# A pool of their own for the last split weights of FFN 1, and the second head's context keys right behind the first head's

## The chip, the cores and the metric

The kernel runs on one core of a Trainium2 chip. The metric is the device time of one execution in microseconds (us). The kernel before took 988.46 us (median of 3 runs, 988.08 to 989.26).

## What is computed

One block over 256 latent tokens (stream x) and 256 context tokens (stream ctx), 1024 channels, float32. The parts that matter here:

```
x   = x   + 0.5 * g1x * swiglu(modulate(rmsnorm(x,   norm_ffn1), sh1x, sc1x), w13_ffn1, w2_ffn1)
ctx = ctx + 0.5 * g1c * swiglu(modulate(rmsnorm(ctx, norm_ffn1), sh1c, sc1c), w13_ffn1, w2_ffn1)
qc, kc, vc, ... = project(modulate(rmsnorm(ctx, norm_mix), sh2c, sc2c), w_in)
qx, kx, vx, ... = project(modulate(rmsnorm(x,   norm_mix), sh2x, sc2x), w_in)
qx, kx = rope_2d(qx, rows), rope_2d(kx, rows)
```

Then come 4 heads of bidirectional retention of the latent queries over context and latent keys, a Fourier branch, a merge, a second FFN on x, and a final norm.

## The kernel before, in words

**Products in three terms.** Each float32 operand is split into a high part (rounded to fp32r) and a low part (the rest). `mm3` (lines 93 to 97) adds three matmuls: low weight by high activation (L95), high by low (L96), high by high (L97). `load_w` (line 77) fetches a chunk of weights (128 x up to 1024) into a raw tile `wr`, ScalarE casts it to `wh` (L85), and VectorE, or GpSimd where the caller asks for it, subtracts to give `wl` (L86). The tags `wr`, `wh` and `wl` have 4 buffers each, so 4 chunks at most are held in split form at one time. `split` (line 89) does the same two steps (L90, L91) for a given destination.

**FFN 1, second half** (`ffn1_down(1, g)`, line 472). Eight feature blocks j are made, each by 33 matmuls of 512 columns with 11 split blocks of weights, which come in two chunks (6 and 5 blocks). The last two, j = 6 and 7, are kept back (`late`) and run stream by stream: for the context columns j = 6 then 7, then for the latent columns j = 6 then 7, 33 matmuls of 256 columns each. So their four split chunks stay in the `wh` and `wl` buffers until the end of this stage, which are all four of each. They are put 16 columns into their buffers (`at`). The norm of the context stream (`stage2_norm(0)`: six matmuls with a matrix of ones, L506 and L508, a square root on ScalarE, L233, a reciprocal on VectorE, L235) is set in after the first blocks of the latent columns.

**Start of the mixers** (lines 857 to 867). `stage2_mod(0, ...)` makes the context's activations `h2ch`/`h2cl` block by block: VectorE multiplies by the norm (L328, writes `xr`), ScalarE adds the shift (L331, the high part), VectorE subtracts (L332, the low part). `first_unit` projects the first head's context keys (tile `kc`, 48 matmuls of 256 columns) and transposes the activations (tile `ht`, L631) block by block. Its hook, after block `HOOK` = 0, emits the latent stream's norm and its 8 activations `h2xh`/`h2xl`. Then `first_unit` does the same for the latent keys (`kx`), `project` makes the first head's queries (`q`), and the second head's latent keys (`kx1`). `k_weights(0)` and `q_weights(0)` give their subtractions to GpSimd (`G`), those of later heads to VectorE.

**The head loop** (lines 869 to 890). For the first head: scores (`s`, 24 matmuls), the second head's latent keys are rotated, then the second head's context keys are projected (line 884, tile `kc`, 48 matmuls), then `u_unit` (which needs the scores after their evacuation into `pt`), then the second head's queries (`q1`), then `o_unit`. `q_evac` (line 717) rotates and splits the queries (L705, L709, L90, L91); the scores need it.

**What sets the order.** Only the opening is ordered by hand. After it, the framework orders each engine's instructions when the kernel is built: by program order as the priority, by readiness in a model of the engines, and by free buffers. The order is then fixed, and each engine works through it and waits where it must.

**Memory.** Pools on the "left" and on the "right" side are two stacks that grow towards each other. In each partition, `gp` on the left ends at byte 178,208, and above it lay `adp` and `adr`, which are closed before this stage. On the right, `dp` ends downward at 206,304, and `mc` (the 16 tiles of 1,024 bytes of `h2ch`/`h2cl`) takes 189,920 to 206,304. A tile that lies over an older one waits for that one's last reader (`reuse_waits="tile"`).

Of the kernel before, what the change touches and what calls it, by code (L numbers as in the profile page):

```python
# [8 lines left out]
F32R = mybir.dt.float32r  # L9
# [4 lines left out]
P = 128  # L14
T = 256
D = 1024
KT = D // P
# [7 lines left out]
HALF = MT // 2  # L25
# [1 line left out]
RAW = 4  # L27
OUT = (P, KT, T)
UB = 4
HOOK = 0  # L30
LINE = 32
TC_KW = dict(schedule_with_timeline_sim=True)

# [6 lines left out]
def block_kernel(ctx: ExitStack, tc: tile.TileContext, i: dict, out: bass.AP):  # L40
    nc = tc.nc
# [10 lines left out]
    def fpool(stack, name, side):  # L52
        return stack.enter_context(tc.tile_pool(name=name, bufs=1, reuse_waits="tile", side=side))
# [7 lines left out]
    def shifted(pool, name, eighths):  # L61

        if eighths:
            V.memset(pool.tile([P, 8 * eighths], F32, name=name), 0.0)

    def bank(name):
        return psum.tile([P, 512], F32, name=name, tag="ps")

    def f32(ap):
        return ap.bitcast(F32)  # L70

    uid = [0]

    def wtile(t, name):
        return wp.tile([P, 1024], F32 if t == "wr" else F32R, name=name, tag=t, bufs=4)

    def load_w(src, n, lo_engine=None, at=0):

        uid[0] += 1
        raw, hi, lo = [wtile(t, f"{t}{uid[0]}")[:, at : at + n] for t in ("wr", "wh", "wl")]  # L80
        dst = raw
        if len(src.shape) == 3:
            dst = dst.rearrange("p (k c) -> p k c", k=src.shape[1])
        nc.sync.dma_start(dst, src)
        S.copy(hi, raw)  # L85
        (lo_engine or V).tensor_tensor(lo, raw, f32(hi), op=ALU.subtract)  # L86
        return hi, lo

    def split(dst_hi, dst_lo, src):
        S.copy(dst_hi, src)  # L90
        V.tensor_tensor(dst_lo, src, f32(dst_hi), op=ALU.subtract)  # L91

    def mm3(o, w, a, start, stop):

        PE.matmul(o, w[1], a[0], start=start, stop=False)  # L95
        PE.matmul(o, w[0], a[1], start=False, stop=False)  # L96
        PE.matmul(o, w[0], a[0], start=False, stop=stop)  # L97

    def sl(pair, *idx):
        return pair[0][idx], pair[1][idx]  # L100
# [13 lines left out]
    pools = {}  # L114
# [227 lines left out]
    def gated_unit(pa, pb, name):  # L342
        sa = tp.tile([P, 512], F32, name=f"sa{name}", tag="t2k", bufs=T2K)
        S.activation(sa, pa, AF.Silu)
        V.tensor_tensor(sa, sa, pb, op=ALU.mult)
        gg = (
            gp.tile([P, 512], F32R, name=f"gh{name}", tag="gh", bufs=HALF),
            gp.tile([P, 512], F32R, name=f"gl{name}", tag="gl", bufs=HALF),
        )
        split(gg[0], gg[1], sa)  # L350
        return gg
# [74 lines left out]
    def some_ada(n):  # L426
        for _ in range(min(n, len(todo))):
            ada(*todo.pop(0))

    def ffn1_up(m):  # L430
# [10 lines left out]
                mm3(ps, sl(ws[k // 4], slice(None), slice(c, c + P)), h[k], k == 0, k == KT - 1)  # L441
        return gated_unit(pa, pb, f"1_{m}")

    def w2_chunks(src, kts, at=0):
        ws, k0 = [], 0
        for n in kts:
            w = load_w(src[:, k0 * P : (k0 + n) * P], n * P, at=at)
            ws += [sl(w, slice(None), slice(c * P, (c + 1) * P)) for c in range(n)]
            k0 += n
        return ws  # L450
# [3 lines left out]
    def add_sq(ap, cols, first, name):  # L454

        sq = tp.tile([P, 512], F32, name=f"sq{name}", tag="t2k", bufs=T2K)
        w = cols.stop - cols.start
        if first:
            S.activation(ssum[0][:, cols], ap, AF.Square)
            return  # L460
        S.activation(sq[:, :w], ap, AF.Square)
        V.tensor_tensor(ssum[0][:, cols], ssum[0][:, cols], sq[:, :w], op=ALU.add)

    def y_evac(ps, j, streams, st, col0):
        for n, s in enumerate(streams):
            c = slice(s * T, (s + 1) * T)
            V.scalar_tensor_tensor(
                xs[j][:, c], ps[:, col0 + n * T : col0 + (n + 1) * T], gate_col(st, s, j),
                xs[j][:, c], op0=ALU.mult, op1=ALU.add,
            )  # L470

    def ffn1_down(hf, gs, n_ada=0):
        late = []
        if hf:
            ssum[0] = per.tile([P, 512], F32, name="ssum2", tag="ssum")
        for j in range(KT):
            some_ada(n_ada)
            in_two = hf and j >= KT - 2
            ws = w2_chunks(i["w2a"][hf, j], (6, 5), 16 if in_two else 0)
            if in_two:  # L480
                late.append((j, ws))
                continue
            ps = bank(f"y{hf}_{j}")
            for k in range(HALF):
                mm3(ps, ws[k], gs[k], k == 0, k == HALF - 1)
            y_evac(ps, j, (0, 1), 0, 0)
            if hf:
                add_sq(xs[j], slice(0, 512), j == 0, f"2_{j}")
        for s in (0, 1):
            for j, ws in late:  # L490
                ps = bank(f"y{hf}_{j}_{s}")
                c = slice(s * T, (s + 1) * T)
                for k in range(HALF):
                    mm3(ps[:, :T], ws[k], sl(gs[k], slice(None), c), k == 0, k == HALF - 1)
                    if (s, j, k) == (1, KT - 2, 3):
                        norms.append(stage2_norm(0))
                y_evac(ps, j, (s,), 0, 0)
                sq = tp.tile([P, T], F32, name=f"sq2_{j}_{s}", tag="t1k", bufs=2)
                S.activation(sq, xs[j][:, c], AF.Square)
                late_sq[s].append(sq)  # L500
# [3 lines left out]
    def stage2_norm(s):  # L504
        ps = bank(f"st2_{s}")
        PE.matmul(ps[:, :T], ones, ssum[0][:, s * T : (s + 1) * T], start=True, stop=False)  # L506
        for n, sq in enumerate(late_sq[s]):
            PE.matmul(ps[:, :T], ones, sq, start=False, stop=(n == 1))  # L508
        return rstd_of(ps[:, :T], T, f"2_{s}")
# [17 lines left out]
    def log_sigmoid():  # L527
# [28 lines left out]
    hx2 = [  # L556
        (mp.tile([P, T], F32R, name=f"h2xh{k}"), mp.tile([P, T], F32R, name=f"h2xl{k}"))
        for k in range(KT)
    ]
# [4 lines left out]
    def decays(hd):  # L564
# [16 lines left out]
    raw = tp.tile([P, P], F32, name="unit_2", tag="t1k", bufs=2)  # L581
    nc.sync.dma_start(raw, i["unit"])
    V.tensor_copy(unit, raw)
    dec = {0: decays(0)}
    S.activation(warm, dec[0][0][:, :1], AF.Sqrt, bias=dec[0][1][:, :1])
    ffn1_down(1, g)
    ffn1.close()
    mc = fpool(heads, "mc", "right")
    hc2 = [
        (mc.tile([P, T], F32R, name=f"h2ch{k}"), mc.tile([P, T], F32R, name=f"h2cl{k}"))  # L590
        for k in range(KT)
    ]
# [23 lines left out]
    def stage2_mod(s, r):  # L616
        for k in range(KT):
            modulated((hc2, hx2)[s][k], 1, (s,), k, r, s * T, f"2_{s}_{k}", None)
# [21 lines left out]
    def first_unit(s, w, a, pss, hook=None):  # L640

        banks = {}
        for k in range(KT):
# [3 lines left out]
            transposed(s, k, banks)  # L647
            if hook and k == HOOK:
                hook()
# [42 lines left out]
    def k_weights(hd):  # L692
        return [load_w(i["wk"][hd, n], 1024, None if hd else G) for n in range(2)]

    def kc_evac(pss, at):
        for e in range(2):
            split(keys[e][0][:, :T], keys[e][1][:, :T], pss[e][:, at[e] : at[e] + T])
# [27 lines left out]
    def project(ws, a, name):  # L725
        ps = bank(name)
        pair_of(ws, a, (ps, ps), (0, T))
        return (ps, ps), (0, T)
# [128 lines left out]
    wk = k_weights(0)  # L857
    stage2_mod(0, norms[0])
    kc = [bank(f"kc0_{e}") for e in range(2)]
    first_unit(0, wk, hc2, kc, lambda: stage2_mod(1, stage2_norm(1)))  # L860
    kc_evac(kc, (0, 0))
    kx = [bank(f"kx0_{e}") for e in range(2)]
    first_unit(1, wk, hx2, kx)
    kx_evac(0, kx, (0, 0))
    q_evac(0, *project(q_weights(0), hx2, "q0"))
    wk = k_weights(1)
    kx = project(wk, hx2, "kx1")
    sq = None
    for hd in range(HEADS):
        last = hd == HEADS - 1  # L870
        score_unit(hd)
        if last:
            fourier_open()
            fourier_in(0)
        else:
            dec[hd + 1] = decays(hd + 1)
            if hd:
                wk = k_weights(hd + 1)
                kx = project(wk, hx2, f"kx{hd + 1}")
            kx_evac(hd + 1, *kx)  # L880
        if hd:
            o_norm(hd - 1, sq)
        if not last:
            kc_evac(*project(wk, hc2, f"kc{hd + 1}"))
        us = u_unit(hd)
        if last:
            fourier_in(1)
        else:
            q_evac(hd + 1, *project(q_weights(hd + 1), hx2, f"q{hd + 1}"))
        sq = o_unit(hd, us)  # L890
# [19 lines left out]
    for j in range(KT):  # L910
        ws = [load_w(i["wgate"][j, c], 1024) for c in range(2)]
# [6 lines left out]
        wr = [load_w(i["pret"][j, c], 1024) for c in range(2)]  # L918
        for k in range(2 * KT):
            c = (k % 8) * P  # L920
# [120 lines left out]
    for j in range(KT):  # L1041
        ws = w2_chunks(i["w2b"][j], (8, 8, 6))
# [6 lines left out]
        if j < KT - 1:  # L1049
            add_sq(xs[j][:, XC], slice(0, T), j == 0, f"4_{j}")  # L1050
            c = NRM + 3 * KT + j
# [5 lines left out]
    c = NRM + 4 * KT - 1  # L1057
# [109 lines left out]
```

## Time and profile before

| what | value |
|---|---|
| median of 3 runs | 988.46 us (988.08 to 989.26) |
| the profiled execution | 986.11 us |
| its span, first to last instruction | 984.3 us |
| TensorE matmul (PE) busy | 957.3 us, 97% |
| VectorE (DVE) busy | 658.1 us, 67% |
| ScalarE (ACT) busy | 468.1 us, 48% |
| GpSimd (POOL) busy | 37.7 us, 4% |
| chain that ended last, PE's share | 93% |

The span is 1.81 us shorter than the profiled execution's own time, and that execution is 2.35 us below the median. A row of the timeline gives the start and the duration in us, the engine, the line, the operation, the tile written and the tiles read, and in brackets how long the engine had been idle and who released it. PE durations overlap from one matmul to the next, so costs of PE are taken from the distance between starts.

### The profile page before, as it was taken

What the parts mean: (1) busy time and instruction counts of PE and PEld (TensorE: products, weight loads), DVE (VectorE), ACT (ScalarE), POOL (GpSimd) and SP (SyncE); (2) the same over time, 40 slices, a digit from 0 to 9 for tenths busy, and PEclk for the clock granted to TensorE, in tenths of its full rate; (3) what the DMA queues carried; (4) which work ended last, traced back from release to release, by engine and by line L of the source; (5) the groups of instructions that cost most, each with busy time, mean ns of one, the idle gap of its engine ahead of it and who ended that gap; (6) DMA issues with size and microseconds to landing.
All of it is one profiled execution on the core that took longest, in us unless ns stands there. A gap on an engine that the chain in (4) does not pass through costs nothing.

```text
span 984.3 us, 16732 instructions
## 1 busy us (share of the span) xinstructions
PE 957.3 (97%) x6792; PEld 881.2 (90%) x6792; DVE 658.1 (67%) x1056; ACT 468.1 (48%) x733; POOL 37.7 (4%) x21
## 2 busy tenths in 40 slices
PE   6999999999999999899999999899999999999996
PEld 4778888888888889899999999899999999999995
DVE  7879999998333433966765646975555688555553
ACT  5444322224422432755665647755444566555541
POOL 0000000000000001200000006200000000000000
PEclk9999999999999999999999999999999999999998
DMA  8757766995332232323231526356656565666661
GB/s 348 238 203 235 235 195 214 352 391 195 97 109 67 78 99 86 97 87 121 95 130 44 157 81 186 117 175 201 192 189 199 174 190 175 211 198 186 199 190 43
DMA packets 49237, 166.84 MB, mean 169 GB/s; under 512 B 5380, under 2 KB 7044, under 8 KB 49160
## 3 DMA queue, kind: packets, MB, share of 16 engines
q1 hardware_dynamic: 49160, 165.77, 52.4%
q8 instruction: 53, 0.87, 0.3%
q14 instruction: 24, 0.20, 0.1%
HBM read 164.70 MB, written 1.05 MB: 168 GB/s over the span
## 4 chain that ended last, share of the span: by engine, by line
PE 93%; DVE 3%; ACT 1%; DMA 1%; issue 1%; DVEq 0%; SPq 0%; ACTq 0%
PE y L95 4%; PE y L97 4%; PE y L96 4%; PE pa L97 4%; PE pb L95 4%; PE pa L95 4%; PE pb L97 4%; PE pa L96 3%; PE pb L96 3%; PE ro L97 2%; PE ro L95 2%; PE ro L96 2%; PE fb L97 2%; PE fa L97 2%; PE fb L96 2%; PE fa L96 2%
## 5 line engine op out<-in xcount | busy, mean ns | idle before, releaser
L86 DVE TENSOR_TENSOR wl<-wr,wh 128x1024 fp32r<-128x1024 f32 (+1 forms) x214 | 248.7, 1163 | 190.4 <-ACT wh L85 189.5
L85 ACT CAST wh<-wr 128x1024 fp32r<-128x1024 f32 (+1 forms) x226 | 227.3, 1007 | 273.7 <-PE y L97 79.2
L198 DVE CUSTOM_DVE_ANT_0 junk<-ada,cb,sm 128x1024 bf16<-128x1024 f32 x96 | 123.0, 1281 | 6.5 <-DMA ada<-in_ada 4.9
L96 PE MATMUL y<-gl,wh 128*128 128x512 f32 (+1 forms) x198 | 72.4, 366 | 0.0
L95 PE MATMUL y<-gh,wl 128*128 128x512 f32 (+1 forms) x198 | 72.3, 366 | 0.0
L97 PE MATMUL y<-gh,wh 128*128 128x512 f32 (+1 forms) x198 | 72.2, 365 | 0.0
L97 PE MATMUL pa<-h1h,wh 128*128 128x512 f32 x152 | 59.2, 389 | 0.0
L96 PE MATMUL pa<-h1l,wh 128*128 128x512 f32 x152 | 59.2, 389 | 0.0
L95 PE MATMUL pa<-h1h,wl 128*128 128x512 f32 x152 | 59.2, 389 | 0.0
L95 PE MATMUL pb<-h1h,wl 128*128 128x512 f32 x152 | 59.2, 389 | 0.0
L96 PE MATMUL pb<-h1l,wh 128*128 128x512 f32 x152 | 59.2, 389 | 0.0
L97 PE MATMUL pb<-h1h,wh 128*128 128x512 f32 x152 | 59.1, 389 | 0.0
L96 PE MATMUL z<-g2l,wh 128*128 128x256 f32 x176 | 48.8, 277 | 0.0
L97 PE MATMUL z<-g2h,wh 128*128 128x256 f32 x176 | 48.6, 276 | 0.0
L95 PE MATMUL z<-g2h,wl 128*128 128x256 f32 x176 | 48.6, 276 | 0.0
L86 POOL TENSOR_TENSOR wl<-wr,wh 128x1024 fp32r<-128x1024 f32 x12 | 29.9, 2515 | 439.2 <-ACT wh L85 439.2
L96 PEld LDWEIGHTS y<-gl,wh 128*128 128x128 f32 x198 | 37.3, 188 | 6.1
L95 PEld LDWEIGHTS y<-gh,wl 128*128 128x128 f32 x198 | 37.2, 188 | 6.0
L97 PEld LDWEIGHTS y<-gh,wh 128*128 128x128 f32 x198 | 37.2, 188 | 6.0
L97 PE MATMUL fb<-hnh,wh 128*128 128x256 f32 x144 | 39.8, 276 | 0.0
L96 PE MATMUL fb<-hnl,wh 128*128 128x256 f32 x144 | 39.8, 276 | 0.0
L97 PE MATMUL fa<-hnh,wh 128*128 128x256 f32 x144 | 39.8, 276 | 0.0
(336 smaller groups left out, 2903.1 us busy)
## 6 DMA issues: line engine op xcount, KB each, us to landing
ada<-in_ada SPq DMA_DIRECT2D x72, 512.0 KB, 5.2
wr<-in_w13b SPq DMA_DIRECT2D x44, 512.0 KB, 4.4
wr<-in_w13a SPq DMA_DIRECT2D x38, 512.0 KB, 4.4
wrv<-in_wv SPq DMA_DIRECT2D x16, 512.0 KB, 4.5
wr<-in_wg SPq DMA_DIRECT2D x16, 512.0 KB, 4.1
wr<-in_wgate SPq DMA_DIRECT2D x16, 512.0 KB, 4.4
wr<-in_pret SPq DMA_DIRECT2D x16, 512.0 KB, 4.1
wr<-in_w2b SPq DMA_DIRECT2D x16, 512.0 KB, 3.8
```

What stands on the lines that cost most here:

```text
L85: S.copy(hi, raw)
L86: (lo_engine or V).tensor_tensor(lo, raw, f32(hi), op=ALU.subtract)
L95: PE.matmul(o, w[1], a[0], start=start, stop=False)
L96: PE.matmul(o, w[0], a[1], start=False, stop=False)
L97: PE.matmul(o, w[0], a[0], start=False, stop=stop)
L198: V.tensor_tensor_reduce(junk, raw, cb[:, s, :], 1.0, sm[:, BIAS + n : BIAS + n + 1], ALU.mult, ALU.add, mod[:, s, n : n + 1],)
```

## The change

`HOOK` goes from 0 to 1. The late blocks j = 6 and 7 of FFN 1 are split into four tiles of a new pool `late` (5,632 bytes each per partition, behind a pad of 320), by way of `wr` as before but without `wh` and `wl`. The new pool is opened on the left before `ffn1_down(1, g)` and closed after it. The second head's key weights are loaded after the first head's context keys, and the second head's context keys `kc1` are projected there, before the first head's latent keys; in the loop the first head's pass only evacuates them.

```diff
-HOOK = 0
+HOOK = 1
...
+    def late_weights(src, j):
+
+        pair = [pools["late"].tile([P, HALF * P], F32R, name=f"late{j}_{x}") for x in range(2)]
+        for k0, k1 in ((0, 6), (6, HALF)):
+            c = slice(k0 * P, k1 * P)
+            uid[0] += 1
+            raw = wtile("wr", f"wr{uid[0]}")[:, : (k1 - k0) * P]
+            nc.sync.dma_start(raw, src[:, c])
+            split(pair[0][:, c], pair[1][:, c], raw)
+        return [sl(pair, slice(None), slice(k * P, (k + 1) * P)) for k in range(HALF)]
...
-            in_two = hf and j >= KT - 2
-            ws = w2_chunks(i["w2a"][hf, j], (6, 5), 16 if in_two else 0)
-            if in_two:
+            if hf and j >= KT - 2:
+                ws = late_weights(i["w2a"][hf, j], j)
+            else:
+                ws = w2_chunks(i["w2a"][hf, j], (6, 5))
+            if hf and j >= KT - 2:
                 late.append((j, ws))
                 continue
...
+    late = ExitStack()
+    pools["late"] = fpool(late, "late", "left")
+    shifted(pools["late"], "pad_late", 10)
     ffn1_down(1, g)
+    late.close()
     ffn1.close()
...
     kc_evac(kc, (0, 0))
+    wk1 = k_weights(1)
+    kc1 = project(wk1, hc2, "kc1")
     kx = [bank(f"kx0_{e}") for e in range(2)]
     first_unit(1, wk, hx2, kx)
     kx_evac(0, kx, (0, 0))
     q_evac(0, *project(q_weights(0), hx2, "q0"))
-    wk = k_weights(1)
-    kx = project(wk, hx2, "kx1")
+    kx = project(wk1, hx2, "kx1")
...
-            kc_evac(*project(wk, hc2, f"kc{hd + 1}"))
+            kc_evac(*(project(wk, hc2, f"kc{hd + 1}") if hd else kc1))
```

## Rows read from the trace of the kernel before

**Rows 1.** The page, busy time and share of the span by engine

```profile
PE 957.3 (97%) x6792; PEld 881.2 (90%) x6792; DVE 658.1 (67%) x1056; ACT 468.1 (48%) x733; POOL 37.7 (4%) x21
```

**Rows 2.** Busy time by stretch: stretch, length, PE, PEld, DVE, ACT, POOL, granted clock, DMA

```profile
396.00:400.00 4.00, 1.09 (x5) 0.66 (x5) 4.00 (x9) 2.01 (x5) 2.13 (x1) 1.00 0.80 240
400.00:404.00 4.00, 3.70 (x17) 3.35 (x18) 4.00 (x6) 1.45 (x3) 2.47 (x1) 0.60 0.27 98
```

**Rows 3.** Timeline of PE, from the end of FFN 1 to the latent keys

```profile
395.31 0.28 PE L97 MATMUL y<-gh,wh 128*128 128x256 f32 x1
396.60 0.47 PE L95 MATMUL kc<-h2ch,wl 128*128 128x256 f32 x2 [1.02 <-ACT h2ch L331]
...
411.32 0.35 PE L95 MATMUL kx<-h2xh,wl 128*128 128x256 f32 x1
```

**Rows 4.** Timeline of DVE, 391 to 403.5 us

```profile
391.46 1.75 DVE L235 RECIPROCAL rstd<-sd 128x256 f32<-128x256 f32 x1 [4.27 <-ACT sd L233]
393.13 0.39 DVE L467 SCALAR_TENSOR_TENSOR xs<-y,gate,xs 128x256 f32<-128x256 f32 x1
393.44 2.48 DVE L328 SCALAR_TENSOR_TENSOR xr<-xs,amul,rstd 128x256 f32<-128x256 f32 x1
395.84 2.57 DVE L328 SCALAR_TENSOR_TENSOR xr<-xs,amul,rstd 128x256 f32<-128x256 f32 x1
398.34 0.47 DVE L328 SCALAR_TENSOR_TENSOR xr<-xs,amul,rstd 128x256 f32<-128x256 f32 x1
...
400.96 2.57 DVE L328 SCALAR_TENSOR_TENSOR xr<-xs,amul,rstd 128x256 f32<-128x256 f32 x1
```

**Rows 5.** Timeline of POOL, its four subtractions of this stage

```profile
390.87 2.40 POOL L86 TENSOR_TENSOR wl<-wr,wh 128x1024 fp32r<-128x1024 f32 x1 [390.43 <-ACT wh L85]
393.23 2.41 POOL L86 TENSOR_TENSOR wl<-wr,wh 128x1024 fp32r<-128x1024 f32 x1
395.58 2.55 POOL L86 TENSOR_TENSOR wl<-wr,wh 128x1024 fp32r<-128x1024 f32 x1
400.77 2.47 POOL L86 TENSOR_TENSOR wl<-wr,wh 128x1024 fp32r<-128x1024 f32 x1 [2.64 <-ACT wh L85]
```

**Rows 6.** Timeline of ACT: casts of weights, and the first context activation

```profile
368.10 0.83 ACT L85 CAST wh<-wr 128x768 fp32r<-128x768 f32 x1 [2.58 <-PE y L97]
...
389.74 1.05 ACT L85 CAST wh<-wr 128x1024 fp32r<-128x1024 f32 x1 [2.09 <-PE y L97]
...
395.95 0.51 ACT L331 ACTIVATE h2ch<-xr,mod 128x256 fp32r<-128x256 f32 x1 [0.97 <-DVE xr L328]
```

**Rows 7.** Timeline of PE, four matmuls of a norm and the next matmul

```profile
387.92 0.60 PE L506 MATMUL st<-ssum,ones 128*128 128x256 f32 x2
...
388.60 0.47 PE L95 MATMUL y<-gh,wl 128*128 128x256 f32 x1
```

**Rows 8.** Busy time of PE by stretch (kx0; q0; kx1; scores with kc1): length, busy, clock, DMA

```profile
411.32:419.89 8.57, 8.57 (x83) 1.00 0.02 4
419.89:425.42 5.53, 5.53 (x52) 1.00 0.49 162
425.42:430.86 5.44, 5.44 (x51) 1.00 0.58 148
430.86:439.29 8.43, 8.43 (x74) 1.00 0.12 47
```

**Rows 9.** Timeline of DVE, the first head's queries

```profile
426.53 1.41 DVE L705 SCALAR_TENSOR_TENSOR qr<-q,rope 128x256 f32<-128x256 f32 x4
427.86 1.22 DVE L86 TENSOR_TENSOR wl<-wr,wh 128x1024 fp32r<-128x1024 f32 x1
...
429.88 0.76 DVE L91 TENSOR_TENSOR qt<-qr,qt 128x256 fp32r<-128x256 f32 x2
```

**Rows 10.** Timeline of PE, the matmul that follows the last score

```profile
435.41 0.28 PE L95 MATMUL kc<-h2ch,wl 128*128 128x256 f32 x1
```

**Rows 11.** Busy time by stretch, a short hole of PE in the Fourier part (columns of Rows 2)

```profile
616.00:618.00 2.00, 0.59 (x5) 0.59 (x6) 1.91 (x3) 2.00 (x3) 1.08 (x1) 1.00 0.54 217
```

## The prediction

> **What bounds the kernel now.** I began with the page: PE is busy for 97% of the span [rows 1], so the time only falls if a hole of PE closes, or its work shrinks. The change removes no matmul, so I looked for holes. The busy time by stretch shows the largest one: from 396 to 400 us PE is busy for 1.09 of 4 us, and in the next 4 us the granted clock is 0.60 on average, a mix of its levels 1.2 and 2.4 GHz [rows 2]. This is the seam between FFN 1 and the mixers. The timeline of PE gives its size: the last matmul of FFN 1 ends at 395.31 + 0.28 = 395.59, the latent keys kx0 start at 411.32 [rows 3], 15.7 us for kc0, 32 transposes and six matmuls of a norm.
>
> Why PE waits there is seen on DVE. The operation L328 takes 0.47 us as a rule, but 2.48, 2.57 and 2.57 us in three places [rows 4], and the first activation on ACT, on which PE waits, follows the first of them [rows 3, 6]. Beside these three stands each time a subtraction of POOL: it runs from 393.23 to 395.64, from 395.58 to 398.13 and from 400.77 to 403.24 [rows 5], and L328 ends each time within 0.3 us after it. L467 at 393.13, which reads PSUM, and the reciprocal take their usual 0.39 and 1.75 us beside POOL [rows 4]. So DVE's operations on two SBUF inputs stand still while POOL subtracts: (2.48 + 2.57 + 2.57) - 3 x 0.47 = 6.2 us of DVE.
>
> And why POOL runs just then: its work waits for a cast on ACT, and that cast waits for PE's y matmuls [rows 6]. All four buffers of wh and wl hold the late blocks, so the first head's key and query weights are split only when these are done with, at the worst moment.
>
> **What the seam costs.** The same 48 matmuls and 32 transposes take 8.57 us for kx0 at full clock [rows 8]. Four matmuls of a norm take 388.60 - 387.92 = 0.68 us [rows 7], six some 1.0. So 9.6 us would do where 15.7 are spent: 6.1 us are lost.
>
> **The change, part by part.**
>
> *The pool for the late blocks.* Loads, casts and subtractions stay as many (four chunks, same queue, same raw buffers); a memset of 0.1 us comes on DVE, far from the path. What moves is the split of the key weights: their wh and wl now come free with block j = 4, whose first chunk is done with near 368 us, where the cast for j = 6 stood [rows 6]. Its two POOL subtractions (4.8 us, rows 5) then run near 370 to 375, where DVE only squares and splits ahead of need. They cost nothing there; if DVE's own splits were held by them, two blocks of 7 us of matmuls still cover it. The second head's key weights follow when j = 5 is done, on ACT and DVE, in the slack before 388.
>
> What is late next: the late pool ends at 178,208 + 320 + 4 x 5,632 = 201,056, and h2ch begins at 189,920. So the first context activations lie over the weights of j = 7 and cannot be written before the last matmul of FFN 1 ends, at 395.59. In the kernel before ACT wrote the first at 395.95. Now: 395.59, 0.1 to the release, 0.51 on ACT, 0.14 to PE (396.46 to 396.60 before, rows 3, 6), so 396.34, and 0.5 for the low part, half of it beside two matmuls. I take 0.9 us of hole. Ends: 0 and the 1.0 us that PE waits here now, as the POOL work is gone. A hole of this size does not lower the clock: between 616 and 618 us PE is busy 0.59 of 2 us and the clock stays at 1.00 [rows 11]. So of 6.1 us lost, 5.2 come back.
>
> *HOOK, and kc1 behind kc0.* The latent norm and its 16 DVE operations are set in one block later. On DVE the seam is now 32 operations at about 0.42 us pitch, a reciprocal of 1.75 and some 1.6 of evacuations, 16.8 us from 393.5 on, so until 410.3. PE has kc0 and the norm until 395.59 + 0.9 + 9.6 = 406.1, and kc1 (48 matmuls, 5.5 us by q0 and kx1, rows 8) until 411.6. The latent activations are there in time; kc1 is the cover, without it PE would wait some us. kx0 then ends at 420.2. Before, it ended at 419.89 with kc1 still to be done: 5.5 - 0.3, the same 5.2 us.
>
> *What kc1 no longer covers.* Two covers are lost, and this is what I subtract.
> First, the query weights. The four buffers now hold both heads' key weights, so the second chunk of q0 can be split only when kx0 ends: 420.2 + 1.05 (cast) + 2.5 (POOL) = 423.8, where before it was there at 403.24 [rows 5, 6]. PE has q0's first quarter (1.4 us) and kx1 (5.44) to do, so it need not stand still, but q0 ends at 423.8 + 4.1 = 427.9, and kx1's rest at 431.1. The scores need the rotated queries: from 425.59 to 430.86 this took 5.3 us, with two splits of 1.2 us between [rows 8, 9]; without them about 3. So the scores start between 431.1 and 433.4: a hole of 0 to 2.3 us, I take 1.2, the middle, since the splits for q1 now come at the same time on DVE.
> Second, the gap between the scores and u. It lasts from 435.41 to 439.29, 3.9 us [rows 8, 10], and kc1 filled it. Only q1 can now. Its buffers come free with kx1 at 431.1, and a cast of 1.05 and a DVE split of 1.22 per chunk put it at 433.4 and 434.6, just ahead of the end of the scores. A hole of 0 to 3.9; I take 0.6, near the lower end, since the weights stand ready by this sum.
>
> POOL's work for q0 also meets the rotation of kx0 on DVE near 421 to 424 and holds up to two of its operations; the keys are needed seven us later, so nothing is charged.
>
> **Sum.** 5.2 - 1.2 - 0.6 = 3.4 us. The profiled execution of 986.11 us would be 982.7. It stands 2.35 below the median, so against the median of 988.46: 985.1. With both covers in full 5.2 us (983.3), and with no wait at the seam 6.1 (982.4); with both holes in full 5.2 - 6.2 = -1.0 (989.5).
>
> **A rule against it.** The trace shows DVE blocked by POOL, and no POOL subtraction drawn out (2.40 to 2.55 us, rows 5). The Trainium skill, "SBUF — State Buffer", section "Who interferes with whom", says that the order of issue decides: a DVE operation with two SBUF inputs that starts first makes GpSimd wait. By it the rotation of kx0 could hold q0's split, which the sum above has as undisturbed.
>
> **Rivals.**
> - *q0 stops PE.* The order is fixed at build time; if it has q0 in one piece ahead of kx1, PE waits from 421.6 to 423.8, and any slip on ACT or POOL is added; then the covers no longer meet their gaps. Holes of 3.2 to 7.2 us: 986.5 to 990.4, the middle 988. For it: q0 precedes kx1 in program order. Against: PE's order now mixes s and kc by readiness [rows 10].
> - *DVE holds POOL.* By that order of issue q0's second chunk starts up to one DVE operation late, 0.4 to 1.2 us (half of L91's pair, or one L86, rows 9), and all of it reaches the scores: 985.5 to 986.3. For it: four such operations (L709 and L91, two each) stand there. Against: POOL was never seen waiting.
> - *Slower: the scores lose both covers.* If PE spends all of kx1 ahead of q0, q0 ends at 431.2 and the rotation stands open, up to 5.3 us; if q1's split is then queued on DVE behind it, the 3.9 us behind the scores are open too. 9.2 - 5.2 = 4.0: 992.5. It decides from 7.2 us of holes on. Against: q1's buffers would then be free early.
> - *Not done.* The key weights' split stays behind the late blocks, because the raw buffers come late or the built order has it so; then kc1 can't help, as it needs the same activations: 988.5. Against: nothing but the blocks j = 4 and 5 then holds these buffers, and the casts follow their release at once [rows 6].
>
> **How the numbers follow.** The forecast has 0.58, DVE holds POOL 0.08, q0 stops PE 0.17, slower 0.11, not done 0.06. About 0.2% (2.0 us) is what a measurement of this kernel tells from no change. Faster by over that: 0.58 + 0.08 = 0.66; within: 0.17 + 0.06 = 0.23; slower 0.11. The range reaches from both covers held with a little of the wait at the seam (983.0) to the upper part of the second case (988.8).
>
> **What would show it.** POOL's first two subtractions near 370 us; L328 at 0.47 us throughout the seam; kc0 from about 396.4 at full clock; kc1 before kx0; kx0 ending near 420; then PE holes of under 2 us before s and u. Wrong if L328 is still drawn out, if ACT's first h2ch waits long after 395.6, or if PE stands still for more than 3 us between 420 and 440.

## The result and the profile after

The changed kernel takes 992.95 us (median of 5 runs, 992.05 to 996.03) where the kernel before took 988.45 in the same runs (5 runs, 988.08 to 989.26): a ratio of 1.0047, 95% interval 1.0035 to 1.0058. It is slower by 4.5 us, where 985.1 was forecast, and lies outside the range.

The profiled execution of the changed kernel took 996.03 us, with a span of 994.3; that of before 986.11, with 984.3. So the two traces differ by 10.0 us of span, more than the medians do. 3.24 of it lies ahead of the change: FFN 1 ends at 398.83 instead of 395.59, since the opening took longer in this execution (in the profiles of this study it ends between 395.59 and 398.83, in no order that follows the edits). From the first matmul of `o` (466.25, before 456.25) to the end both take 528.05 us. So the whole effect lies between the end of FFN 1 and `o`: 67.42 us, before 60.66. I read it there, in two halves.

**The seam.** First the page's line on the engines [rows 1], then the timelines of POOL [rows 5], of DVE [rows 4], of ACT [rows 6] and of PE [rows 3] in the changed kernel, and its busy time by stretch (columns of rows 2).

```profile
PE 965.0 (97%) x6792; PEld 888.4 (89%) x6792; DVE 656.1 (66%) x1057; ACT 468.7 (47%) x733; POOL 37.5 (4%) x21
```

```profile
372.47 2.39 POOL L86 TENSOR_TENSOR wl<-wr,wh 128x1024 fp32r<-128x1024 f32 x1 [372.03 <-ACT wh L85]
375.87 2.39 POOL L86 TENSOR_TENSOR wl<-wr,wh 128x1024 fp32r<-128x1024 f32 x1 [1.01 <-ACT wh L85]
420.49 2.40 POOL L86 TENSOR_TENSOR wl<-wr,wh 128x1024 fp32r<-128x1024 f32 x1 [42.23 <-ACT wh L85]
424.03 2.48 POOL L86 TENSOR_TENSOR wl<-wr,wh 128x1024 fp32r<-128x1024 f32 x1 [1.15 <-ACT wh L85]
```

```profile
396.68 1.66 DVE L328 SCALAR_TENSOR_TENSOR xr<-xs,amul,rstd 128x256 f32<-128x256 f32 x4
```

```profile
398.86 1.71 ACT L331 ACTIVATE h2ch<-xr,mod 128x256 fp32r<-128x256 f32 x4 [1.59 <-PE y L97]
```

```profile
399.51 0.48 PE L95 MATMUL kc<-h2ch,wl 128*128 128x256 f32 x2 [0.69 <-ACT h2ch L331]
...
423.74 0.35 PE L95 MATMUL q<-h2xh,wl 128*128 128x256 f32 x1
```

```profile
398.83:402.40 3.57, 2.89 (x21) 2.69 (x22) 3.54 (x13) 2.98 (x8) 0.00 (x0) 1.00 0.01 2
```

POOL's first two subtractions have moved from 391 to 372 us. Four L328 take 1.66 us together, where single ones took 2.57. ACT has its inputs, but is released by PE's last `y`: this is the new wait, as `h2ch` lies over the weights of j = 7. PE waits for it for 0.69 us, and the clock stays at 1.00 behind it. From the end of FFN 1 to the first matmul of `q` it takes 423.74 - 398.83 = 24.9 us with kc1 in it; before, 24.3 without kc1, which is some 5.6 us. The seam gives back 5.0 us.

**Behind kx0.** From the first matmul of `q` to `o` it takes 42.5 us; before 36.4, of which kc1 was 5.6. So 42.5 - 30.8 = 11.7 us are lost here. The waits of PE between 380 and 470 us, the steps of PE's timeline, and the busy time by stretch (columns of rows 2):

```profile
PE s L95 <- ACT qt L90: 2.7, 2, 2.5
PE u L95 <- ACT pt L90: 2.6, 1, 2.6
PE kc L95 <- ACT h2ch L331: 0.7, 1, 0.7
```

```profile
425.22 0.28 PE L95 MATMUL kx<-h2xh,wl 128*128 128x256 f32 x1
...
429.11 0.28 PE L95 MATMUL q<-h2xh,wl 128*128 128x256 f32 x1
...
433.35 0.28 PE L95 MATMUL kx<-h2xh,wl 128*128 128x256 f32 x1
...
437.77 0.50 PE L95 MATMUL s<-qt,kt 128*128 128x256 f32 x2 [2.49 <-ACT qt L90]
...
446.60 0.79 PE L95 MATMUL u<-pt,ht 128*128 128x256 f32 x2 [2.63 <-ACT pt L90]
```

```profile
437.80:441.00 3.20, 2.89 (x12) 2.13 (x13) 3.00 (x6) 2.69 (x5) 0.00 (x0) 0.64 0.66 178
441.00:444.00 3.00, 2.96 (x14) 2.67 (x13) 1.90 (x4) 0.96 (x3) 0.00 (x0) 0.50 0.80 229
444.00:446.60 2.60, 0.00 (x1) 0.00 (x1) 2.60 (x7) 2.59 (x4) 0.00 (x0) 0.50 0.32 124
446.60:449.00 2.40, 2.40 (x11) 2.40 (x12) 2.40 (x6) 1.85 (x4) 0.00 (x0) 0.50 0.00 0
449.00:451.00 2.00, 2.00 (x11) 2.00 (x11) 1.81 (x5) 0.15 (x1) 0.00 (x0) 0.50 0.00 0
451.00:453.00 2.00, 2.00 (x14) 2.00 (x13) 0.43 (x1) 0.25 (x1) 0.00 (x0) 0.66 0.00 0
453.00:455.00 2.00, 2.00 (x19) 2.00 (x19) 0.00 (x0) 0.00 (x0) 0.00 (x0) 1.00 0.00 0
```

Two holes of PE stand there, in front of `s` and of `u`: 2.7 + 2.6 = 5.3 us. And behind the first hole the granted clock falls to 0.50, the lower of its levels (1.2 GHz), and is back at 1.00 (2.4 GHz) only after 452 us. Busy time times what is missing of the clock gives 2.89 x 0.36 + (2.96 + 2.40 + 2.00) x 0.50 + 2.00 x 0.34 = 5.4 us. Holes and clock make 10.7 of the 11.7; the rest I could not place.

The timeline of PE also shows why the first hole is there. The second chunk of q0's weights is split by 424.03 + 2.48 = 426.51, but PE does kx1 until 429.11, q0 from there on, and only the last two microseconds of kx1 are left when the queries are done at 433.5. DVE then needs until 437.8 for the rotation (L722 and L726 are L705 and L709 of the kernel before), with the splits of q1's weights in it:

```profile
433.26 1.23 DVE L86 TENSOR_TENSOR wl<-wr,wh 128x1024 fp32r<-128x1024 f32 x1 [5.56 <-ACT wh L85]
434.40 1.41 DVE L722 SCALAR_TENSOR_TENSOR qr<-q,rope 128x256 f32<-128x256 f32 x4
435.73 1.21 DVE L86 TENSOR_TENSOR wl<-wr,wh 128x1024 fp32r<-128x1024 f32 x1
436.86 0.42 DVE L726 TENSOR_TENSOR qr<-qr 128x256 f32<-128x256 f32 x1
```

So q1's weights stand ready at 436.94, ten microseconds ahead of `u`. But the order built for PE has q1 behind the first four matmuls of `u` (its first matmul starts at 447.61), and PE stands still in front of them.

### The profile page after: what moved, and what is told of

It reads as the page before. It is cut to its first block, busy times and chain, and to the rows that moved or that the text cites. A ratio compares the mean times of both kernels' runs of the same rounds, so it can differ in the third digit from the quotient of the medians.

```text
span 994.3 us, 16730 instructions
## 1 busy us (share of the span) xinstructions
PE 965.0 (97%) x6792; PEld 888.4 (89%) x6792; DVE 656.1 (66%) x1057; ACT 468.7 (47%) x733; POOL 37.5 (4%) x21
## 4 chain that ended last, share of the span: by engine, by line
PE 93%; ACT 2%; DVE 2%; DMA 1%; issue 1%; DVEq 0%; SPq 0%; ACTq 0%
PE y L96 4%; PE y L97 4%; PE y L95 4%; PE pa L96 3%; PE pb L96 3%; PE pa L95 3%; PE pb L97 3%; PE pa L97 3%; PE pb L95 3%; PE ro L96 2%; PE ro L95 2%; PE ro L97 2%; PE fb L96 2%; PE fa L96 2%; PE fa L95 2%; PE fb L95 2%
## 5 line engine op out<-in xcount | busy, mean ns | idle before, releaser
L86 DVE TENSOR_TENSOR wl<-wr,wh 128x1024 fp32r<-128x1024 f32 (+1 forms) x210 | 244.8, 1167 | 186.1 <-ACT wh L85 185.3
L85 ACT CAST wh<-wr 128x1024 fp32r<-128x1024 f32 (+1 forms) x222 | 224.2, 1011 | 272.3 <-PE y L97 66.9
L96 PE MATMUL y<-gl,wh 128*128 128x512 f32 x154 | 59.9, 389 | 0.0
L97 PE MATMUL y<-gh,wh 128*128 128x512 f32 x154 | 59.9, 389 | 0.0
L95 PE MATMUL y<-gh,wl 128*128 128x512 f32 x154 | 59.8, 389 | 0.0
L95 PE MATMUL fb<-hnh,wl 128*128 128x256 f32 x144 | 39.7, 276 | 0.0
L95 PE MATMUL fa<-hnh,wl 128*128 128x256 f32 x144 | 39.6, 276 | 0.0
L96 PE MATMUL fa<-hnl,wh 128*128 128x256 f32 x144 | 39.6, 276 | 0.0
```

## The experiments

My theory after the two traces: the pool keeps its gain, and the early kc1 loses more than that, by the two covers it takes away and by the clock. Its rivals: the pool's gain hangs on kc1 as the cover for the latent activations; only the late split of q0 costs anything; the holes are cheap and the clock is the price; the seam would be as well served by another engine. The table holds every run: its median beside the median of before from the same session, and, from its trace, the end of FFN 1 and the time from there to the first `o`, which is free of the opening's spread.

| kernel | median us | before | ratio, 95% | FFN 1 ends | to `o` |
|---|---|---|---|---|---|
| before | | 988.45 | | 395.59 | 60.66 |
| changed | 992.95 | 988.45 | 1.0047 [1.0035, 1.0058] | 398.83 | 67.42 |
| late_only | 983.58 | 988.24 | 0.9955 [0.9941, 0.9968] | 396.48 | 55.78 |
| kc1_only | 997.51 | 988.24 | 1.0089 [1.0075, 1.0103] | 397.22 | 70.95 |
| idle_mm | 989.98 | 988.24 | 1.0014 [1.0006, 1.0023] | 396.69 | 63.15 |
| q1_early | 991.44 | 988.24 | 1.0026 [1.0015, 1.0037] | 397.36 | 62.89 |
| late_swap | 982.51 | 988.21 | 0.9948 [0.9931, 0.9965] | 396.61 | 55.75 |
| wk1_early | 986.32 | 988.21 | 0.9977 [0.9967, 0.9986] | 397.19 | 58.63 |
| q0_first | 990.65 | 988.21 | 1.0025 [1.0015, 1.0035] | 395.85 | 63.49 |
| before_dve | 987.92 | 988.21 | 0.9997 [0.9988, 1.0007] | 396.59 | 60.89 |
| wk1_twice | 989.31 | 988.15 | 1.0015 [1.0004, 1.0026] | 398.58 | 63.22 |
| late_swap_h0 | 983.77 | 988.15 | 0.9951 [0.9939, 0.9964] | 398.61 | 55.78 |

**late_only**: the changed kernel with kc1 and its weights back where they were; the pool and `HOOK` = 1 stay.

```diff
-    wk1 = k_weights(1)
-    kc1 = project(wk1, hc2, "kc1")
...
-    kx = project(wk1, hx2, "kx1")
+    wk = k_weights(1)
+    kx = project(wk, hx2, "kx1")
...
-            kc_evac(*(project(wk, hc2, f"kc{hd + 1}") if hd else kc1))
+            kc_evac(*project(wk, hc2, f"kc{hd + 1}"))
```

> The change without the move of kc1: the late pool and HOOK = 1 stay, the second head's context keys are projected in the loop as before. Theory A (the pool frees the seam, the move of kc1 opens the holes behind kx0 and lowers the clock there): the seam keeps its 4.9 us, no hole behind kx0, kx0 follows kc0 without a wait, since in the changed kernel the first latent activations were ready 10.4 us after the end of FFN 1 and kc0 ends 11.0 us after it: 988.45 - 4.9 = 983.5. Theory B (kc1 is the cover that the latent activations need, as the prediction had it): PE waits 2 to 4 us in front of and within kx0: 985.5 to 987.5. Theory C (the late pool itself costs, by its reuse of memory or by its loads): 988.5 or more.

983.58 us, 4.7 below before. Its only wait of PE between 380 and 500 us, then POOL's last two subtractions, DVE's last low parts of the latent activations, and the steps of PE:

```profile
PE kc L95 <- ACT h2ch L331: 0.7, 1, 0.7
```

```profile
377.61 2.39 POOL L86 TENSOR_TENSOR wl<-wr,wh 128x1024 fp32r<-128x1024 f32 x1 [1.64 <-ACT wh L85]
381.01 2.40 POOL L86 TENSOR_TENSOR wl<-wr,wh 128x1024 fp32r<-128x1024 f32 x1 [1.01 <-ACT wh L85]
```

```profile
412.17 0.88 DVE L332 SCALAR_TENSOR_TENSOR h2xl<-xr,mod,h2xh 128x256 fp32r<-128x256 f32 x2 [0.89 <-ACT h2xh L331]
```

```profile
407.34 0.47 PE L95 MATMUL kx<-h2xh,wl 128*128 128x256 f32 x2
...
415.90 0.35 PE L95 MATMUL q<-h2xh,wl 128*128 128x256 f32 x1
```

The pool alone has the whole gain. q0's weights are now split by 381.01 + 2.40 = 383.4 as well, so nothing is missing behind kx0. And kc1 was never needed as a cover: kx0 begins at 407.34, when DVE is far from done with the latent activations (413.05), and waits for none of them, as it takes them block by block.

**kc1_only**: the other half, the kernel before with kc1 moved (and `HOOK` = 1), without the pool.

```diff
+    wk1 = k_weights(1)
+    kc1 = project(wk1, hc2, "kc1")
...
-    wk = k_weights(1)
-    kx = project(wk, hx2, "kx1")
+    kx = project(wk1, hx2, "kx1")
...
-            kc_evac(*project(wk, hc2, f"kc{hd + 1}"))
+            kc_evac(*(project(wk, hc2, f"kc{hd + 1}") if hd else kc1))
```

> The move of kc1 and HOOK = 1 without the late pool: the late blocks go through the four buffers of wh and wl as before. Theory A: the holes behind kx0 and the lower clock stay (some 11.8 us), and the seam gives back only a part, as the first head's two POOL subtractions still meet DVE there and only q0's two move away: 988.45 + 11.8 - 2 to 4 = 996 to 998. Theory C (the late pool costs): faster than the whole change, 988 to 990.

997.51 us, as expected: 9.3 above before. Its waits of PE show the same two holes, beside those of the seam (1.3 and 1.0 us), which without the pool are still there:

```profile
PE u L95 <- ACT pt L90: 2.6, 1, 2.6
PE s L95 <- ACT qt L90: 2.5, 1, 2.5
```

The two parts add up: -4.7 and +9.3 give +4.6, where both together give +4.5.

**idle_mm**: the changed kernel with 22 matmuls that nobody reads in front of the scores and 22 in front of `u`. They keep PE at work in the holes and bring no result nearer.

```diff
+    def idle(name, n, a):
+        ps = bank(name)
+        for _ in range(n):
+            PE.matmul(ps[:, :T], unit, a, start=True, stop=True)
...
+        if not hd:
+            idle("idle0", 22, hx2[0][0])
...
+        if not hd:
+            idle("idle1", 22, probs[1][0][:, :T])
```

> The whole change plus 22 matmuls of 256 columns into an unread bank in front of the first head's scores and 22 in front of its u, 2.5 us each: the holes of PE (2.5 and 2.6 us) are filled with work that nobody needs. Theory A1 (the holes lower the clock, and that costs 5.4 us beside them): the clock stays at 1.00 through the stage, scores take 2.8 us instead of 6.2: 993.0 - 5.4 = 987.6, within 1.5 us. Theory A2 (the holes alone cost, the clock falls for another reason): 993 to 995, scores still at half the clock.

989.98 us: 3.0 below the changed kernel, less than expected. Busy time by stretch:

```profile
433.00:436.80 3.80, 3.80 (x30) 3.38 (x28) 3.60 (x9) 3.59 (x12) 0.00 (x0) 1.00 0.65 182
436.80:440.20 3.40, 2.62 (x19) 2.20 (x18) 3.37 (x7) 1.92 (x6) 0.00 (x0) 1.00 0.60 208
```

The clock now holds, and the trace takes 63.15 us to `o` where the changed kernel's took 67.42. It holds in the other executions too: the mean granted clock is 0.995 to 0.998 in the eleven of idle_mm, 0.990 to 0.993 in the five of the changed kernel. No result comes earlier for an idle matmul, so what came back is the clock: 3.0 us of the medians, 4.3 of the traces. The split is not exact, as PE still waits 0.3, 0.4 and 0.6 us beside the idle matmuls. So the clock is a real part of the price. The 6.4 us of the medians that remain against late_only are the gaps, with what the idle matmuls hold up; in the medians the gaps are the larger part, in the changed kernel's trace both are about the same (5.3 and 5.4).

**q1_early**: the changed kernel with the second head's queries projected ahead of the first scores, to give the rotation a cover.

```diff
+    q1 = project(q_weights(1), hx2, "q1")
...
-            q_evac(hd + 1, *project(q_weights(hd + 1), hx2, f"q{hd + 1}"))
+            q_evac(hd + 1, *(project(q_weights(hd + 1), hx2, f"q{hd + 1}") if hd else q1))
```

> The whole change, with the second head's queries q1 (48 matmuls, 5.5 us) projected in front of the first head's scores instead of behind u. Theory A1: q1 covers the wait for the rotated queries, the scores start some 3 us later than in the changed kernel but at full clock; the gap in front of u stays open, 2.6 to 3.9 us, and is too late to lower the clock for long: 993.0 - 2.5 - 4 to 5 + 0 to 1.3 = 986 to 988. Theory A2 (the clock falls whatever fills the hole): 990 or more.

991.44 us, a miss for theory A1. The number is theory A2's, the reason is not: where q1 fills the hole in front of the scores the hole is gone and the clock stays at 1.00 (440.00 to 442.40 us). But `u` now has nothing at all in front of it, and the clock falls there (timeline of PE, then busy time):

```profile
447.09 0.80 PE L95 MATMUL u<-pt,ht 128*128 128x256 f32 x2 [4.67 <-ACT pt L90]
```

```profile
447.10:450.00 2.90, 2.78 (x11) 2.49 (x12) 2.90 (x8) 1.44 (x3) 0.00 (x0) 0.50 0.76 264
```

48 matmuls moved from one gap to the other cover one gap less. This is the change itself once more, on a smaller scale.

**wk1_early**: kc1 back in the loop, but the second head's key weights still loaded and split early, so that q0's are late. **wk1_twice**: kc1 early as in the change, but its weights loaded and split a second time for kx1, so that q0's are not late (two more loads, casts and subtractions, none on PE). Against the changed kernel, wk1_early first:

```diff
-    kc1 = project(wk1, hc2, "kc1")
...
-            kc_evac(*(project(wk, hc2, f"kc{hd + 1}") if hd else kc1))
+            kc_evac(*project(wk if hd else wk1, hc2, f"kc{hd + 1}"))
```

and for wk1_twice

```diff
-    kx = project(wk1, hx2, "kx1")
+    kx = project(k_weights(1), hx2, "kx1")
```

> The whole change, but kc1 is projected in the loop as before; only its weights are loaded and split early, so both heads' key weights hold the four buffers and q0's second chunk still comes after kx0. Theory A1 (what costs is that kc1 no longer covers the rotation and the scores; q0's late split only reorders PE's work): no hole of over 0.5 us, clock at 1.00: 983.6 to 984.6. Theory A3 (q0's late split itself costs): a hole of 1 to 3 us in front of q0's rest or of the scores: 985 to 988.

> The whole change, but the second head's key weights are loaded and split a second time for kx1. So kc1 gives its two buffers back when it is done, before kx0 ends, and q0's weights are split early as before; kc1 is still behind kc0 and covers nothing later. Two more loads, casts and subtractions fall where ACT and DVE have slack. It is the fourth corner beside late_only (neither, 983.6), wk1_early (q0's split late, kc1 late: 986.3) and the whole change (both, 993.0). Theory A1 (the missing cover in front of u costs by itself): no hole in front of q0 or the scores, a hole of 3 to 4.2 us in front of u with 2 to 4 us of half clock behind it: 983.6 + 4 to 6 = 987.5 to 989.5. Rival (q0's late split is the root, and without it q1 covers u): 984 to 985.

wk1_early took 986.32 us, above what theory A1 asked for and within A3's range: the late split costs by itself. Its one large wait of PE, and the clock around it:

```profile
430.36 0.50 PE L95 MATMUL s<-qt,kt 128*128 128x256 f32 x2 [2.50 <-ACT qt L90]
```

```profile
427.90:430.36 2.46, 0.00 (x0) 0.00 (x0) 2.33 (x6) 0.45 (x2) 0.00 (x0) 1.00 0.75 213
430.36:433.00 2.64, 2.64 (x22) 2.64 (x23) 0.75 (x2) 0.29 (x1) 0.00 (x0) 1.00 0.65 199
```

wk1_twice took 989.31 us, as expected. It has no hole in front of the scores and the largest one in front of `u`:

```profile
442.51 0.79 PE L95 MATMUL u<-pt,ht 128*128 128x256 f32 x2 [4.19 <-ACT pt L90]
```

```profile
444.00:448.00 4.00, 4.00 (x20) 4.00 (x20) 3.30 (x9) 0.00 (x0) 0.00 (x0) 0.50 0.28 115
```

With late_only and the changed kernel these two make a square, each median against its own before: neither -4.7, q0's weights late -1.9, kc1 early +1.2, both +4.5. So the late weights cost 2.8 us, the missing kc1 5.8, and both together 9.2, little more than their sum of 8.6. The corners are medians of wide runs (wk1_twice 987.59 to 993.05), so the sum is rough; the holes are plain. Each has its own cause: the late split opens the one in front of the scores, kc1's absence the one in front of `u`.

**q0_first**: the changed kernel with kx1 queued on PE behind all of q0, which is the order that the prediction had taken for granted up to a quarter.

```diff
-        PE.matmul(o, w[0], a[0], start=False, stop=stop)
+        return PE.matmul(o, w[0], a[0], start=False, stop=stop)
...
-                mm3(o, sl(ws[k // 4], slice(None), slice(c, c + P)), a[k], k == 0, k == KT - 1)
+                last_mm[0] = mm3(o, sl(ws[k // 4], slice(None), slice(c, c + P)), a[k], k == 0, k == KT - 1)
...
-    kx = project(wk1, hx2, "kx1")
+    with tc.issue_after(last_mm[0].ins):
+        kx = project(wk1, hx2, "kx1")
```

> The whole change, with the matmuls of kx1 queued behind all of q0's on PE. Theory A1: PE waits some 1.2 us for q0's second chunk, then kx1 covers the rotation of the queries, no hole in front of the scores; the gap in front of u stays, some 3 us, and may lower the clock for 2 to 4 us behind it: 988.2 - 4.9 + 4.5 to 7.5 = 988 to 991. Rival (the order of kx1 and q0 does not matter): 993, as the whole change.

990.65 us, as expected. PE waits 1.2 us for POOL's split of q0, none before the scores, and then:

```profile
440.87 0.58 PE L95 MATMUL u<-pt,ht 128*128 128x256 f32 x1 [4.19 <-ACT pt L90]
```

The order of q0 and kx1 is worth 2.3 us of the medians, 992.95 to 990.65 (each against a before that moved by 0.24). It does not save the change. That q1 queued ahead of `u` would fill the second gap was not run.

**before_dve**: the kernel before with the first head's four subtractions on DVE instead of POOL. If the seam's price is that POOL blocks DVE, this takes the block away.

```diff
-        return [load_w(i["wk"][hd, n], 1024, None if hd else G) for n in range(2)]
+        return [load_w(i["wk"][hd, n], 1024) for n in range(2)]
...
-        return [load_w(i["wq"][hd, n], 1024, None if hd else G) for n in range(2)]
+        return [load_w(i["wq"][hd, n], 1024) for n in range(2)]
```

> The kernel before, with the four subtractions of the first head's key and query weights on VectorE instead of GpSimd. Theory P (VectorE stands still while GpSimd subtracts): L328 at 0.47 us throughout; VectorE gets 4.9 us of subtractions of its own, two of them before the norm is ready and two within the seam: the seam loses 2 to 4 us instead of 6.1: 988.2 - 2 to 4 = 984 to 986. Rival (the seam waits for the split weights themselves, whoever makes them): 988 or more.

987.92 us, no different from before, where theory P asked for 984 to 986. DVE and PE in the seam:

```profile
394.93 1.22 DVE L86 TENSOR_TENSOR wl<-wr,wh 128x1024 fp32r<-128x1024 f32 x1
396.06 1.67 DVE L328 SCALAR_TENSOR_TENSOR xr<-xs,amul,rstd 128x256 f32<-128x256 f32 x4
397.64 1.22 DVE L86 TENSOR_TENSOR wl<-wr,wh 128x1024 fp32r<-128x1024 f32 x1
```

```profile
398.13 0.50 PE L95 MATMUL kc<-h2ch,wl 128*128 128x256 f32 x2 [1.54 <-ACT h2ch L331]
401.09 0.58 PE L96 MATMUL kc<-h2cl,wh 128*128 128x256 f32 x1 [1.39 <-DVE h2cl L332]
```

L328 takes its usual time again, 1.67 for four, so it was POOL that drew it out. But the subtractions now stand in DVE's own order ahead of L328 and L332, and the holes stay. What costs is that weights are split at this moment, on whichever engine; what helps is to split them earlier, and for that buffers must be free earlier.

**late_swap** and **late_swap_h0**: late_only with the tiles of j = 7 below those of j = 6 in the pool, so that the first context activations no longer lie over the last weights; the second also with `HOOK` = 0.

```diff
+    def late_tiles(j):
+        return [pools["late"].tile([P, HALF * P], F32R, name=f"late{j}_{x}") for x in range(2)]
...
-        pair = [pools["late"].tile([P, HALF * P], F32R, name=f"late{j}_{x}") for x in range(2)]
+        pair = pools[j]
...
+    for j in (KT - 1, KT - 2):
+        pools[j] = late_tiles(j)
```

> The late pool without the move of kc1 (as late_only, 983.6), with the tiles of j = 7 put below those of j = 6, so that the context activations lie over the weights of j = 6, which are done with 3.9 us before the end of FFN 1. Theory A (the 0.7 us that PE waits at the seam are the wait for the last reader of j = 7): the first activation is written some us before the end of FFN 1, PE goes on without a wait: 983.6 - 0.7 to 0.9 = 982.8. Rival (the wait is ACT's own pace or the low part on DVE): 983.6, the same wait.

> late_swap (982.5) with HOOK = 0 as before, so that the latent norm and its eight activations are set in one block earlier. Theory: the order of DVE in the seam changes by a few operations, the latent activations had slack: the same within 0.5 us, 982.0 to 983.0. Rival (HOOK = 1 is needed, the reciprocal of 1.75 us on DVE holds the context's low parts): a wait of up to 1.7 us of PE within kc0: 983 to 984.5.

982.51 us, the lowest median of the study, and 983.77 us; neither is to be told from late_only's 983.58. late_swap's number is theory A's, its trace is the rival's (the low part on DVE): ACT's wait for the last `y` is gone, and PE's hole is as large as before, one step later:

```profile
397.83 0.39 PE L96 MATMUL kc<-h2cl,wh 128*128 128x256 f32 x1 [0.86 <-DVE h2cl L332]
```

DVE reaches L332 only behind the evacuation of the last `y` and four memsets. From FFN 1's end to `o` all three kernels take 55.75 to 55.78 us, so neither the placing of the tiles nor `HOOK` has a visible effect. The profiled executions of the two differ by 1.94 us, and their FFN 1 ends 2.00 us apart, so what sets them apart lies in the opening.

## Why the prediction was wrong

- **The seam: right.** DVE was held by POOL, POOL's work moved to where it was forecast (370 to 375 us, measured 372.47 to 378.26 with FFN 1 ending 3.24 later), `h2ch` over j = 7's tiles became the new wait (0.9 charged, 0.69 measured), and the sum of 5.2 us came out (5.0 in the trace, 4.7 in late_only's median). kx0 ends where forecast: 420.2 + 3.24 = 423.4, measured 423.74.
- **"kc1 is the cover, without it PE would wait some us": wrong.** I set the end of DVE's 16.8 us against the start of kx0, but kx0 needs its activations one by one over 8.6 us. late_only shows no wait. This step did not enter the sum, but it hid that the pool alone was the better change.
- **The hole before the scores: mis-sized.** 1.2 taken of 0 to 2.3, measured 2.7. The step that failed is that q0 "ends at 423.8 + 4.1 = 427.9", as if PE took up q0 the moment its weights were split: with the later end of FFN 1 that is 431.1, measured 433.5. The split was even earlier than forecast (426.51 against 423.8 + 3.2 = 427.0), but the built order spends two thirds of kx1 (425.22 to 429.11) before it goes back to q0. So kx1 is 3.9 us of cover in front of q0's weights, which needed less, and 1.9 for the rotation, where the sum had 2.2 and 3.2. The rotation itself took 4.3 us from q0's end to the scores; behind 3.2 us of kx1 the hole would have been 1.1, close to the 1.2 taken. (The sum's upper end is a little high: 427.9 + 5.3 = 433.2, so 2.1 and not 2.3.)
- **The hole before `u`: mis-sized, the larger error of the two holes.** 0.6 taken of 0 to 3.9, measured 2.6 behind scores at half clock, and 4.2 to 4.7 behind scores at full clock (wk1_twice, q0_first, q1_early). "The weights stand ready by this sum" was right (436.94, forecast 434.6 + 3.2 = 437.8). But a filler that is ready does not fill when the built order has it behind the waiting instruction. The upper end of 3.9 was nearer the mark. The step that failed is the choice of the lower end: it looked at when q1's weights are ready, and not at where q1 stands in PE's order.
- **The clock: a missing term.** I took a hole of 1.64 us that left the clock alone [rows 11] for the seam, and charged nothing for holes up to 2.3 and 3.9 us elsewhere. It cost 3.0 us by idle_mm's medians, 5.4 in the profiled execution. Yet [rows 2] had the case in front of me: a clock of 0.60 behind a hole.
- **The rivals.** "The scores lose both covers" (992.5, chance 0.11) is nearest to what happened, though only in part by its own mechanism: q0 ended behind two thirds of kx1, not all of it, and q1's split was not late; PE's order put q1 behind `u`. Its holes were smaller than the 9.2 us (5.3), and the clock, which it did not have, made up the difference, so that its time is close is half luck. "q0 stops PE" was not built; q0_first builds it, with holes of 1.2 and 4.2 us, together within the 3.2 to 7.2 named, and 990.65 us, just above its 990.4.
- **"POOL was never seen waiting": wrong.** [Rows 5] had it already: the two subtractions of 2.55 and 2.47 us, where the others take 2.40 and 2.41, began 0.34 and 0.26 us before the end of an L328 and an L332 on DVE. In the changed kernel the one at 424.03 began 0.22 us before the end of DVE's first L726 and took 2.48 us instead of 2.39; in wk1_early it began 0.34 us before and took 2.60 (timeline of POOL):

```profile
417.85 2.60 POOL L86 TENSOR_TENSOR wl<-wr,wh 128x1024 fp32r<-128x1024 f32 x1 [1.22 <-ACT wh L85]
```

  So each engine holds the other, and the one that comes second waits: DVE's second L726 then took 2.63 us instead of 0.4. This agrees with the Trainium skill's order of issue ("SBUF — State Buffer", "Who interferes with whom"). "DVE holds POOL" was right in kind, but it cost 0.1 us here, not 0.4 to 1.2. "Not done" fell with POOL's first row.

In the profiled executions the sum now reads 5.0 - 2.7 - 2.6 - 5.4 - 1.0 (not placed) = -6.7 us, in the medians -4.5. The mean granted clock of the changed kernel's five runs is 0.990 to 0.993, and the profiled one, the slowest of the five, has 0.990. That it stood longer at half clock than the others would explain it, but is only argued.

## What to carry to other kernels

A filler that is moved forward is taken from the gap it covers: before moving one, list every gap that it fills and what is left for each, in the order that is built and not by what would be ready. Price a gap without cover at its full length, and look whether a stretch at half clock has to be added behind it. And when a change has two parts, ask what each does alone: here the pool gives 4.7 us, and the early keys, meant to go with it, take 9.

## What the runs showed of the hardware that was not expected

- **Holes and the granted clock.** A hole of 2.50 us before the scores left the clock at 1.00 (wk1_early). One of 2.49 us was followed by 0.50 from about 439 to 452 us (the changed kernel, the second hole included), and in kc1_only, again 2.49 us, the clock fell within the hole (0.96 over 438.70 to 441.30, 0.50 from there), before anything had followed it. Holes of 4.19 to 4.67 us were followed by 0.50 for 3 to 6 us each time. So neither the length of the hole nor what follows it decides alone. It may also differ between executions of one kernel: the profiled one of wk1_early has a mean clock of 0.998, the highest of its eleven, which go down to 0.994. What decides stays open. The same holes with idle matmuls in them left 1.00.
- **A part of the gap before `u` is ACT's own order.** Between the two casts of `pt` in the changed kernel stand a load of an activation table and the activation behind it on the same line (timeline of ACT, then of DVE):

```profile
443.02 0.62 ACT L90 CAST pt<-sc 128x512 fp32r<-128x512 f32 x1 [2.53 <-DVE sc L759]
...
443.93 1.28 ACT L582 ACT_TABLE_LOAD   x1
445.22 0.81 ACT L582 ACTIVATE da<-dist,bi,lg 128x512 f32<-128x512 f32 x1
445.94 0.60 ACT L90 CAST pt<-sc 128x512 fp32r<-128x512 f32 x1
```

```profile
444.28 0.68 DVE L759 TENSOR_TENSOR sc<-s,dec 128x512 f32<-128x512 f32 x1
```

That is 1.28 + 0.81 us of work for the next head's decay ahead of the cast that `u` waits for. Not all of it lengthens the gap: DVE has the cast's input ready only at 444.96, so ACT's order costs at most 445.94 - 444.96 = 1.0 us here. It stands there in the kernel before as well, where kc1 hid it. Moving it behind the second cast was not tried.
